# Layer 0's first stage, one k tile at a time: squares on TensorE, a third a_u head inside, and three queues ordered by hand

## The chip, the cores and the metric

The kernel runs on 1 core of one Trainium2 chip. The metric is the device time of one execution in microseconds (us). Several executions are timed, and their median is given; one more execution was recorded by the hardware profiler.

## The reference

A two-layer trunk over a latent stream x (256 tokens) and a context (256 tokens), width 2048, everything in float32. What matters here is the beginning of a layer:

```python
for l in range(DEPTH):                                   # DEPTH = 2
    shift, scale, gate = split(silu(c) @ w_mod[l] + b_mod[l], 3)        # latent
    shift_c, scale_c, gate_c = split(silu(c_ctx) @ w_mod[l] + b_mod[l], 3)   # context
    h   = rmsnorm(x,   g_pre[l]) * (1 + scale)   + shift
    h_c = rmsnorm(ctx, g_pre[l]) * (1 + scale_c) + shift_c
    proj, proj_c = h @ w_in[l], h_c @ w_in[l]            # 5120 columns: a_u a_v a_g b_q b_k b_v b_g c_x c_g
    # branch A: gelu(a_u) * (w_s-mixing of rmsnorm(gelu(a_v))) * silu(a_g)   (4 heads of 128)
    # branch B: windowed attention;  branch C: Fourier mixing;  each times its own silu gate
    y = rmsnorm(concat(branches) @ w_out[l], g_post[l])
    x = x + gate * y                                     # and the context likewise, but in the last layer
```

`rmsnorm` divides by the root of the mean of squares over the 2048 channels, plus 1e-6.

## The kernel before

**Layout.** Channels lie on the 128 partitions: x and the context together are 16 tiles `yo[k]` of 128 channels by 512 tokens (256 latent, 256 context), one for each k tile of the contraction. Products that must be accurate are done in three passes (`mm3`): both operands are split into a rounded part and the rest (`hi` by a copy on ScalarE, `lo` by a subtraction on VectorE), and hi·hi, hi·lo, lo·hi are added up in PSUM. Weights come as half tiles of 128 x 1024 f32 (512 KB) in the order of a list (`Stream`, object `W`): `W.emit` loads one into a `raw` buffer (three of them) and splits it into `whi` and `wlo` (four of each); `W.next` hands out the next one.

**Modulation.** Shift and scale of layer 0 are needed before any h. `mod_start(k0, nk)` computes them for `nk` k tiles: it loads the columns of `w_mod` that belong to them in four parts (`kg`), multiplies with silu(c) held in `cpad` (f32 products, each on 32 columns of TensorE's array, four column groups side by side, `tile_position`), transposes the result on VectorE, and sums and spreads it by four small products (`modc`). VectorE then writes scale (`gs`) and shift (`sh`). The weights of the modulation, 2 MB for a k tile, are the larger part of what the first stage loads. They lie in buffers that are free so early: `hh8`..`hl15` for pairs, `mraw macc vv mg mgl yo0`..`yo3` for single tiles.

**First stage.** `layer(0)` begins with a stage that runs over k, not over output columns, because h comes one k tile after the other: for each k, all of a_v (four blocks of 128 tokens by 512 columns, 12 products) and two heads of a_u (6 products) are added up in six PSUM banks; two further banks (`ms`) serve everything small. The eight first k tiles are taken in four pairs (`blocks`, `PAIRS`), the other eight singly. In each block: make h for its tiles (`prep_h`, `make_h`: scale on VectorE, add shift and round on ScalarE, rest on VectorE), then the products, and between them the pieces of `mod_start` of the next block.

Ahead of it: x is loaded, ScalarE squares each tile (`add_sq`), VectorE adds the squares up in `acc0`, TensorE sums over channels (`col_sums`), VectorE and GpSimd form one over the root (`rstd_cols`), VectorE makes diagonal matrices of it (`rstd_diag`), TensorE spreads it over the partitions (`bcast`), and VectorE copies it to `rb0`.

After the first stage come units (`tunit`), each a head of 128 output columns with 48 products: a_u's heads 2 and 3, then c_x, a_g, and so on. Branch A's elementwise work, the Fourier work and the attention are generators (`later`), which are stepped when a sum of modelled product times has reached their due time. The rest of the modulation (`mods`) is done on VectorE in pieces, at a rate set for each phase (`RATE`, `pace`).

**What sets the order.** TensorE's instructions are in program order (`tc.manual_schedule`); the other engines' and the load queue's order is made by a scheduler from priorities and due times.

## Time and profile before

| | |
|---|---|
| median of 3 runs | 1156.88 us (1156.8 to 1158.5) |
| the profiled execution | 1158.18 us |
| its span in the profile | 1156.4 us |
| TensorE busy (products) | 1126.6 us, 97% of the span |
| VectorE busy | 893.5 us, 77% |
| ScalarE busy | 520.0 us, 45% |
| GpSimd busy | 31.7 us, 3% |
| read from HBM | 231.08 MB, written 2.10 MB |

In the profile PE is TensorE's products, PEld its weight loads, DVE is VectorE, ACT ScalarE, POOL GpSimd, SP SyncE, whose queue issues the loads. A row of a timeline has the start and the length in us, the engine, the line of the kernel, the operation, output and inputs by the program's names, shapes, and a count (x). An f32 product appears as two records. Ends of products are modelled: starts are the surer measure. What ended an engine's idle time stands in brackets.

### The profile page before, as it was taken

To read this page: it belongs to the slowest core of one execution; us is meant where nothing else is said; L and a number is where in the kernel's file an instruction comes from. 1 tells how busy PE (TensorE), PEld (TensorE's weight loads), DVE (VectorE), ACT (ScalarE), POOL (GpSimd) and SP (SyncE) were. 2 spreads that over 40 slices of the span, in tenths; PEclk is the share of its full clock that TensorE was granted. 3 is DMA by queue.
4 is the path that set the end of the run, shared out by engine and by line. 5 is a ranking of instruction groups with operands and counts; after the bars stand their busy time and mean duration, and the time that the engine had idled before them with its cause. 6 is when DMAs were issued, how large, how long until landed. Compare 5 with 4: busy or idle time off the path is not lost.

```text
span 1156.4 us, 16569 instructions
## 1 busy us (share of the span) xinstructions
PE 1126.6 (97%) x6146; PEld 927.1 (80%) x6146; DVE 893.5 (77%) x1503; ACT 520.0 (45%) x950; POOL 31.7 (3%) x39
## 2 busy tenths in 40 slices
PE   3999999999999999999999999999999999999996
PEld 1466688888898888888888888888888988888875
DVE  5454498788988678798999897386988689868775
ACT  4222523322234676642523323366664369856442
POOL 0000000000000000000000000200500000000001
PEclk9999999999999999999999999999999999999999
DMA  9999765455665334345656665356956666556973
GB/s 341 377 391 348 258 209 164 155 182 182 212 207 182 108 104 162 102 165 181 200 164 211 221 205 194 101 164 207 219 164 202 209 209 191 173 165 205 308 251 110
DMA packets 75681, 234.27 MB, mean 203 GB/s; under 512 B 8784, under 2 KB 11984, under 8 KB 75600
## 3 DMA queue, kind: packets, MB, share of 16 engines
q1 hardware_dynamic: 73296, 231.11, 60.0%
q0 software_dynamic: 2304, 2.10, 1.2%
q8 instruction: 48, 0.79, 0.3%
q14 instruction: 33, 0.27, 0.1%
HBM read 231.08 MB, written 2.10 MB: 202 GB/s over the span
## 4 chain that ended last, share of the span: by engine, by line
PE 95%; DMA 2%; DVE 1%; ACT 1%; issue 0%; SPq 0%; POOL 0%; DVEq 0%; POOLq 0%; ACTq 0%
PE ps_t L384 15%; PE ps_t L385 15%; PE ps_t L386 15%; PE ps_t L496 11%; PE ps_t L497 5%; PE ps_mod L172 3%; PE ps_y L385 2%; PE ps_y L386 2%; PE ps_av L384 2%; PE ps_y L384 2%; PE ps_av L385 2%; PE ps_av L386 2%; PE ps_tp L759 1%; PE ps_v L386 1%; PE ps_v L384 1%; PE ps_v L385 1%
## 5 line engine op out<-in xcount | busy, mean ns | idle before, releaser
L367 ACT CAST whi<-raw 128x1024 fp32r<-128x1024 f32 x218 | 228.3, 1051 | 381.2 <-PE ps_t L385 231.1
L368 DVE TENSOR_TENSOR wlo<-raw,whi 128x1024 fp32r<-128x1024 f32 x218 | 265.0, 1219 | 76.0 <-ACT whi L367 75.0
L384 PE MATMUL ps_t<-hh,whi 128*128 128x512 f32 (+1 forms) x784 | 301.0, 384 | 0.0
L386 PE MATMUL ps_t<-hh,wlo 128*128 128x512 f32 (+1 forms) x784 | 299.4, 382 | 0.0
L385 PE MATMUL ps_t<-hl,whi 128*128 128x512 f32 (+1 forms) x784 | 299.1, 382 | 0.0
L209 DVE SCALAR_TENSOR_TENSOR macc<-mraw,cs,macc 128x512 f32<-128x512 f32 x360 | 249.5, 744 | 13.3 <-DMA mraw<-in_wmod_dram 13.1
L496 PE MATMUL ps_t<-hh,whi 128*128 128x512 f32 x512 | 185.6, 400 | 0.0
L386 PEld LDWEIGHTS ps_t<-hh,wlo 128*128 128x128 f32 x784 | 147.3, 188 | 29.3
L384 PEld LDWEIGHTS ps_t<-hh,whi 128*128 128x128 f32 x784 | 147.4, 188 | 29.1 <-issue 1.5
L385 PEld LDWEIGHTS ps_t<-hl,whi 128*128 128x128 f32 x784 | 147.4, 188 | 27.3 <-issue 0.2
L497 PE MATMUL ps_t<-hh,wlo 128*128 128x256 f32 x512 | 143.5, 280 | 0.0
L496 PEld LDWEIGHTS ps_t<-hh,whi 128*128 128x128 f32 x512 | 96.2, 188 | 21.4 <-issue 0.2
L497 PEld LDWEIGHTS ps_t<-hh,wlo 128*128 128x128 f32 x512 | 96.7, 189 | 0.3 <-issue 0.2
L463 ACT ACTIVATE hh<-w2k,sh 128x256 fp32r<-128x256 f32 x48 | 21.7, 501 | 56.6 <-DVE w2k L459 56.6
L384 PE MATMUL ps_y<-whi,hh 128*128 128x512 f32 x112 | 46.2, 412 | 0.0
L385 PE MATMUL ps_y<-wlo,hh 128*128 128x512 f32 x112 | 43.8, 392 | 0.8 <-DVE tot L905 0.8
L386 PE MATMUL ps_y<-whi,hl 128*128 128x512 f32 x112 | 43.8, 392 | 0.0
L384 PE MATMUL ps_av<-whi,hh 128*128 128x512 f32 x96 | 40.0, 417 | 0.0
L385 PE MATMUL ps_av<-wlo,hh 128*128 128x512 f32 x96 | 37.9, 395 | 0.4 <-DVE wlo L368 0.4
L172 PE MATMUL ps_mod<-hh,kt 128*32 128x512 f32 x64 | 21.6, 649 | 16.9 <-DMA hh<-in_wss_dram 16.9
L477 DVE TENSOR_TENSOR acc<-acc,w2k 128x512 f32<-128x512 f32 (+1 forms) x33 | 21.1, 641 | 18.8 <-ACT w2k L476 17.3
L401 ACT CAST w2k<-ps_tp 128x512 fp32r<-128x512 f32 x40 | 23.3, 583 | 22.0 <-PE ps_scc L385 12.0
(336 smaller groups left out, 1704.6 us busy)
## 6 DMA issues: line engine op xcount, KB each, us to landing
raw<-in_win_dram SPq DMA_DIRECT2D x160, 512.0 KB, 3.7
mraw<-in_wmod_dram SPq DMA_DIRECT2D x128, 512.0 KB, 4.2
raw<-in_wout_dram SPq DMA_DIRECT2D x64, 512.0 KB, 4.3
hh<-in_wss_dram SPq DMA_DIRECT2D x32, 256.0 KB, 5.7
hl<-in_wss_dram SPq DMA_DIRECT2D x32, 256.0 KB, 5.6
yo<-in_xT_dram SPq DMA_DIRECT2D x16, 256.0 KB, 5.3
mraw<-in_wsl_dram SPq DMA_DIRECT2D x8, 512.0 KB, 6.5
yo<-in_wsl_dram SPq DMA_DIRECT2D x16, 256.0 KB, 6.4
```

The source lines that it names most:

```text
L172: PE.matmul(ps[32 * kk:32 * kk + 32, 0:n], cpad[:, kg * 4 + kk], ws[kk], start=kg == 0, stop=kg == 3, tile_position=(0, 32 * kk))
L209: V.scalar_tensor_tensor(out=acc[:, s], in0=w[:, kk % 2], scalar=c, in1=acc[:, s], op0=ALU.mult, op1=ALU.add)
L367: A.copy(ph, r[:, c])
L368: self.last = V.tensor_tensor(out=pl, in0=r[:, c], in1=ph.bitcast(F32), op=ALU.subtract)
L384: PE.matmul(ps, st[0], mv[0], start=start, stop=False)
L385: PE.matmul(ps, st[0], mv[1], start=False, stop=False)
L386: PE.matmul(ps, st[1], mv[0], start=False, stop=stop)
L401: A.copy(hi, src)
L463: first = A.activation(h_of(l, k, sl)[0], t[:, sl], AF.Identity, bias=sh[l][:, k, s:s + 1])
L477: V.tensor_tensor(out=acc[:, sl], in0=acc[:, sl], in1=q[:, sl], op=ALU.add)
L496: PE.matmul(ps, w[0], h, start=k == 0, stop=False)
L497: PE.matmul(ps[:, 0:S], w[1], h[:, 0:S], start=False, stop=k == KT - 1)
```

## The change

- **Single tiles.** Layer 0's first stage takes all 16 k tiles singly. Modulation for k+1 is computed in step k; odd tiles below 8 use `hh14 hl14 hh15 hl15` beside `mg mgl`.
- **Third a_u head.** The unit au2 leaves the list behind the stage. Its two half tiles come inside (placed in `hh12 hl12 hh13 hl13` and `yo4`..`yo7`), and it is added up in one of the two `ms` banks: 21 products a step instead of 18. For k = 0, 1, 2 its products come together at the end of step 2. Branch A takes the three heads together, and its due times are changed.
- **Squares.** ScalarE squares each x tile, TensorE sums it over the channels (one product on 32 columns, four column groups in turn), with no addition on VectorE. The reciprocal root is spread by four products whose stationary side is one column repeated, so the diagonals go (in layer 1 too).
- **Products of zeros** (`warm`): bf16, 128 x 512, results unused: one ahead of each square's product, and groups of 2, 2, 3 and 4 up to the first step, 3 and 6 in step 0.
- **Order by hand.** VectorE, ScalarE and the load queue run in program order until the last product group of a_v at k = 14. x comes first in the queue (ahead of the constants and vectors). Loads of weights (`LOADS`) and their splits (`SPLITS`) are counted out step by step; the first split of a step is cut in two, its second part behind h. In steps 0 to 4 the modulation products lie within the step, from step 5 (`NEXT`) at its beginning.

```diff
-PAIRS, ALONE = [0, 2, 4, 6], list(range(8, KT))
+PAIRS, ALONE = [0], list(range(KT))
...
+    wz = sb([P, T], BF16, "join", 2)
+    def warm(ps, n):
+        for _ in range(n):
+            PE.matmul(ps, wz[:, 0:P], wz, start=True, stop=True)
-    def bcast(dg, n):
+    def bcast(r, n):
         ps = ms_ps("rb")
-        PE.matmul(ps[:, 0:n * P], ones, dg.rearrange("p a b -> p (a b)"), start=True, stop=True)
+        for j in range(n):
+            PE.matmul(ps[:, j * P:(j + 1) * P], r[:, j:j + 1].to_broadcast([P, P]), ident, start=True, stop=True)
...
-    NEAR = [1] * 6 + [0] * 6 + [1, 2, 3]
+    NEAR = [0] * 14 + [1, 2, 3]
+    LOADS = [1, 1, 1, 2, 1, 1, 1, 1, 1, 0, 2, 0, 1, 1, 1, 0]
+    SPLITS = [1, 1, 1, 2, 0, 1, 0, 2, 1, 1, 0, 2, 0, 1, 1, 1]
+    MIDDLE, NEXT = 3, 5
...
-        au = [mm_ps("au") for _ in range(2)]
+        au = [mm_ps("au") for _ in range(2)] + [ms_ps("au") for _ in range(1 - l)]
...
+        if l == 0:
+            for k in range(KT):
+                m = mod_start(k + 1, 1) if k + 1 < KT else iter([None] * 4)
+                def mods_next():              # modulation products of k+1, then LOADS[k] loads
...
+                def h_next():                 # modc, scale and shift, h of k+1, SPLITS[k] splits
...
+                if k % 2 == 0:
+                    take(k)
+                if k >= NEXT:
+                    mods_next()
+                    start_av(k, range(nt))
+                    if k == KT - 2:
+                        first_stage.close()
+                    h_next()
+                    if k >= KT - 2:
+                        for _ in range(2):
+                            with low(LAG), tc.issue_after(W.last.ins):
+                                next(mods)
+                    take(k, (1, 2))
+                    start_au(k)
+                elif k == 0:
+                    start_av(0, range(nt))
+                    mods_next()
+                    warm(au[2], 3)
+                    h_next()
+                    warm(au[2], 6)
+                    take(0, (1,))
+                    start_au(0, (0, 1))
+                elif k < MIDDLE:
+                    start_av(k, range(nt))
+                    take(k, (1,))
+                    start_au(k, (0,))
+                    mods_next()
+                    start_au(k, (1,))
+                    h_next()
+                    if k == 2:
+                        ws_[2] = W.next()
+                        for i in range(k + 1):
+                            start_au(i, (2,))
+                else:
+                    start_av(k, range(nt // 2))
+                    mods_next()
+                    start_av(k, range(nt // 2, nt))
+                    h_next()
+                    take(k, (1,))
+                    start_au(k)
...
-        raw = w2k([P, NFIRST])
-        DMA.dma_start(raw, const[:, 0:NFIRST])
...
-        for k in range(KT):
-            add_sq(acc0, yo[k], FULL, k == 0)
-        m = mod_start(*blocks[0])
-        next(m)
-        ps = ms_ps("rs")
-        col_sums(ps, acc0, 4)
-        dg = rstd_diag(ps[:, 0:4], 4, D)
...
+        first_stage.enter_context(tc.manual_schedule(engines={EN.DVE, EN.Activation, EN.SP}))
+        DMA.dma_start(ct, cT)
+        for k in range(KT):
+            DMA.dma_start(yo[k], xT[k])
+        raw = w2k([P, NFIRST])
+        DMA.dma_start(raw, const[:, 0:NFIRST])
+        DMA.dma_start(vecs, vec)
...
+        sq, idle = mm_ps("rs2"), mm_ps("idle")
+        for k in range(KT):
+            q = w2k([P, T])
+            A.activation(q, yo[k], AF.Square)
+            warm(idle, 1)
+            c = slice(32 * (k % 4), 32 * (k % 4) + 32)
+            PE.matmul(sq[c], ones[:, 0:32], q, start=k < 4, stop=k >= KT - 4, tile_position=(0, 32 * (k % 4)))
...
+        m = mod_start(0, 1)
+        next(m)
+        warm(idle, 2)
+        ps = ms_ps("rs")
+        for j in range(4):
+            PE.matmul(ps[:, j:j + 1], row[:, j * P:(j + 1) * P], cc("sel")[:, 0:1], start=True, stop=True)
+        r0 = rstd_cols(ps[:, 0:4], 4, D)
+        next(m)
+        warm(idle, 2)
+        rb = bcast(r0, 4)
+        rb0 = sb([P, T], F32, "acc")
+        A.copy(rb0, rb)
...
+        warm(idle, 3)
+        list(m)
+        warm(idle, 4)
```

## The prediction

> **What bounds the kernel now.** I read first the page of the profile, then the chain of waits up to 60 us, then TensorE's timeline.

> ```profile
> span 1156.4 us, 16569 instructions
> ...
> PE 95%; DMA 2%; DVE 1%; ACT 1%; issue 0%; SPq 0%; POOL 0%; DVEq 0%; POOLq 0%; ACTq 0%
> ```

> The chain of work is TensorE almost throughout. What the change touches lies ahead of that:

> ```profile
> 5.95 5.40 DMA yo<-in_xT_dram
> 11.37 5.41 DMA hh<-in_wss_dram
> 16.92 3.85 PE ps_mod L172 x8
> ...
> 31.74 5.55 PE ps_mod L172 x16
> 37.29 0.43 PE ps_av L384
> ```

> The columns are start, length, what. Until 37.3 us the chain is x arriving, the first modulation weights arriving (11.37 to 16.9), and modulation products paced by arriving weights (31.74, 5.55 us); only then does the first a_v product run. From there TensorE paces the stage:

> ```profile
> 88.43 0.50 PE L384 MATMUL ps_av<-whi,hh 128*128 128x512 f32 x1
> ...
> 91.09 0.40 PE L386 MATMUL ps_av<-whi,hl 128*128 128x512 f32 x1
> 91.42 0.24 PE L182 MATMUL ps_modc<-w2k,cst 128*32 128x4 f32 x8
> 91.60 0.50 PE L384 MATMUL ps_au<-hh,whi 128*128 128x512 f32 x1
> ...
> 92.86 0.40 PE L386 MATMUL ps_au<-hh,wlo 128*128 128x512 f32 x1
> 93.19 1.07 PE L172 MATMUL ps_mod<-mraw,kt 128*32 128x256 f32 x16
> ...
> 94.51 0.61 PE L172 MATMUL ps_mod<-vv,kt 128*32 128x256 f32 x8
> 95.05 0.50 PE L384 MATMUL ps_av<-whi,hh 128*128 128x512 f32 x1
> 95.39 0.39 PE L385 MATMUL ps_av<-wlo,hh 128*128 128x512 f32 x1
> ...
> 127.93 0.50 PE L384 MATMUL ps_av<-whi,hh 128*128 128x512 f32 x1
> ...
> 137.11 0.50 PE L384 MATMUL ps_t<-hh,whi 128*128 128x512 f32 x1
> ```

> One step over a k tile goes from one first a_v product to the next: 88.43 to 127.93 are six steps, 6.58 us each, with 18 products (12 a_v, 6 a_u) 0.23 us apart (88.43 to 91.09), the small group that spreads the modulation (91.42) and 16 modulation products (93.19 to 95.05). The stage ends at 137.11, where the unit of the third a_u head begins. No gap in these rows is a wait for data, so here more bandwidth is worth nothing, and an earlier first a_v product is worth its whole amount.

> The profiled execution took 1158.18 us, its span 1156.4; the median of the runs is 1156.88. The sum below is made on the profiled one; the forecast is 1.3 lower, for the median.

> **Work moved inside, and what is saved.** The third head adds 3 products per k tile, 48 in all, 48 x 0.23 = 11.0 us, and its unit behind the stage, also 48, goes. So TensorE's total stays, and the old stage to be compared ends at 137.1 + 11.0 = 148.1. The new step is 6.58 + 0.69 = 7.27 us; fifteen, and a last one of 21 x 0.23 = 4.8 without modulation, make 113.9 us. Two tiles of modulation that ran ahead of the first a_v product now run behind it: that is in the count.

> The order inside a step decides whether the making of h hides. From the small group to the new hi and lo parts:

> ```profile
> 20.99 1.03 PE L429 MATMUL ps_rs<-ones,acc 128*128 128x1 f32 x8
> ```
> ```profile
> 126.95 1.05 PE L172 MATMUL ps_mod<-yo,kt 128*32 128x256 f32 x16
> ...
> 130.88 0.24 PE L182 MATMUL ps_modc<-w2k,cst 128*32 128x4 f32 x8
> ```
> ```profile
> 22.05 0.16 DVE L412 TENSOR_SCALAR rs_a<-ps_rs 128x4 f32<-128x4 f32 x1 [2.97 <-PE ps_rs L429]
> ```
> ```profile
> 22.30 1.03 POOL L414 TENSOR_TENSOR rs_b<-rs_a,mhalf 128x4 f32<-128x4 f32 x1 [21.85 <-DVE rs_a L412]
> ```
> ```profile
> 143.05 0.58 ACT L401 CAST mg<-ps_mg 128x512 fp32r<-128x512 f32 x1
> ```
> ```profile
> 112.64 1.22 DVE L368 TENSOR_TENSOR wlo<-raw,whi 128x1024 fp32r<-128x1024 f32 x1
> 113.78 0.87 DVE L467 SCALAR_TENSOR_TENSOR hl<-w2k,sh,hh 128x256 fp32r<-128x256 f32 x2
> ...
> 128.07 0.45 DVE L177 STREAM_TRANSPOSE w2k<-ps_mod 128x256 f32<-128x256 f32 x1 [1.12 <-PE ps_mod L172]
> 131.19 0.16 DVE L191 SCALAR_TENSOR_TENSOR gs<-ps_modc,vecs 128x2 f32<-128x2 f32 x1 [2.68 <-PE ps_modc L182]
> ...
> 131.58 0.88 DVE L459 SCALAR_TENSOR_TENSOR w2k<-yo,gs,w2k 128x256 f32<-128x256 f32 x2
> ```

> From 130.88 (small group) scale and shift take until 131.58, the two multiplications 0.88 until 132.46. The change puts half a weight split between them and the lo part (a whole one is 1.22 us at 112.64 and delayed the lo part to 113.78; half is 0.62 by estimate): 133.08, then half of the lo part's 0.88. So the third product of the next a_v can go 2.7 us behind the small group, and an unbroken stream counts as starting 2.25 behind it. From k=5 on, 9 a_u products (2.07) and the modulation group lie between: hidden. For k=3 and 4 the 9 a_u products just do. For k=0, 1 and 2 the order puts modulation ahead of the small group: behind k=1 nothing is left, 2.05 us stand open; behind k=2 the nine postponed third-head products first wait for their own split, 1.75; behind k=0 the zero products fill, yet a_u waits for its split, and the small group for the transpose (0.7 from the end of the modulation products, 126.95 + 0.87, to 128.52), 2.2 in all. Six us of open chain; were half of it covered, 3. Stage length from the first a_v product: 113.9 + 6.0 = 119.9. So the change breaks even if the first a_v product comes at 28.2; it is at 37.3 now.

> **When the first a_v product comes.** Squares are now summed by TensorE: per x tile one product of zeros over the whole array (bf16, 512 columns) and one f32 product on 32 columns. What the latter takes:

> ```profile
> 31.64 1.02 PE L172 MATMUL ps_mod<-hh,kt 128*32 128x512 f32 x2
> ```
> ```profile
> 140.80 1.72 PE ps_mg L646 x4
> ```

> The modulation product at 31.64 is of that shape and alone: two records, 1.02 with its tail. Two f32 products of 512 columns take 1.72, 0.86 each. A one-pass product of 512 is 0.23. Going between the two shapes costs 0.10 in (92.86 to 93.19, less 0.23), 0.11 out (94.51 plus two records of 0.215, to 95.05) and up to 0.11 more on the next product (95.05 to 95.39). So a tile costs 0.86 + 0.23 + 0.2 = 1.29 us; 1.09 if going between is free, 1.41 with all of it. The four column groups, which run four modulation products in 0.43 us at 94.51, don't help here, because a product over all columns stands between any two.

> The trace has no such alternation; I take 1.29 because both shapes stand in it. [...]

> x itself comes faster than that:

> ```profile
> 1.19 0.42 SPq L96 DMA_DIRECT2D vecs<-in_vec_dram  x1
> ...
> 2.12 8.93 SPq L1054 DMA_DIRECT2D yo<-in_xT_dram  x16
> ```
> ```profile
> 5.93 0.63 ACT L473 ACTIVATE acc<-yo 128x512 f32<-128x512 f32 x1 [1.76 <-DMA yo<-in_xT_dram]
> ...
> 7.37 9.47 ACT L476 ACTIVATE w2k<-yo 128x512 f32<-128x512 f32 x14 [0.15 <-DMA yo<-in_xT_dram]
> ```

> Its squares on ScalarE run 0.68 us apart (14 in 9.47). The first square began 3.81 after its issue (2.12 to 5.93); x is now second in the queue, at 1.19, so the first square ends near 1.19 + 3.81 + 0.63 = 5.6. Sixteen tiles at 1.29 are 20.6 us, and TensorE is the slow side; ScalarE waits for it by its seven buffers.

> The clock comes on top:

> ```profile
> 24.00:25.00 1.00, 0.62 (x1) 0.50 (x2) 0.24 (x2) 0.00 (x0) 0.00 (x0) 0.61 1.03 410
> 25.00:26.00 1.00, 1.00 (x2) 0.00 (x0) 0.00 (x0) 0.46 (x1) 0.00 (x0) 0.50 1.03 404
> 26.00:27.00 1.00, 1.00 (x5) 0.20 (x8) 0.53 (x1) 0.76 (x2) 0.00 (x0) 0.50 1.04 385
> 27.00:28.00 1.00, 1.00 (x9) 0.24 (x2) 1.00 (x2) 0.87 (x1) 0.00 (x0) 0.68 1.05 387
> ```

> The third number from the end is the granted clock (behind it the share of the DMA engines and GB/s): 0.61, 0.50, 0.50, 0.68, after a pause of TensorE; it took some 3.4 us of work to come back. The modulation products of 16.92 (four in 3.85 us) were also slow. At half clock 3.4 us lose 1.7; if the work begins inside such a stretch, up to 6.8 us lose 3.4; I take 2.5. [...]

> So the squares end at 5.6 + 20.6 + 2.5 = 28.7 (at best 5.0 + 17.4 + 1.7 = 24.1, at worst 5.6 + 22.6 + 3.4 = 31.6). Behind them, in a row: copy of the sums 0.2 + 0.58 (143.05), four one-column products 1.1 (20.99), rstd on VectorE and GpSimd 1.3 (22.05 to 23.33), four products that spread it, 1.2 by the same row, two groups of modulation 1.0, transpose 0.65, hand-over 0.15, and the 2.25 above: 8.4. First a_v product: 37.1, where it was. What the single tiles gained, the squares take.

> **The sum.** 37.1 + 119.9 = 157.0 against 148.1: 8.9 us longer, 1167.1 for the profiled execution, 1165.8 for the median; as the open chain is counted in full, I say 1165.5. Ends of this case: 24.1 + 8.4 + 116.9 = 149.4 (+1.3, 1158.2) and 31.6 + 8.4 + 119.9 = 159.9 (+11.8, 1168.7).

> **Other edits, priced at nothing.** The 15 additions on VectorE, and the diagonal of rstd, go; their place is the chain above, already counted. In layer 1 one more small product replaces two VectorE multiplications, with products queued behind it. SyncE's queue is now written by hand: loads of the next weights wait in it behind modulation loads, which wait for TensorE to free their buffers; with the first a_v product this late each set has two steps, 14 us, for 2.6 MB (6.7 at the 387 GB/s of the last row above), so it is no bound; were the start early, it would be (below). Two more pieces of the later modulation per end step run on VectorE at low priority. If their cover is gone, a piece costs its own few us once.

> **Rivals.** *The squares hide.* The column groups go on running beside the zero products, the sums keep x's 0.68 us, and end near 17. [...] Then the weights decide: first modulation weights began landing at 16.92 and 1.8 MB more at 387 GB/s land at 21.6; with the last group 0.5, transpose 0.65, hand-over 0.15 and 2.25 the first a_v product is at 25.2. Steps then keep 7.27 against 6.7 of loads: end at 25.2 + 117.9, two us of open chain now lying under loads that must be awaited anyway: 143.1, 5 us sooner, 1152 (1149 to 1155). For it: every early number of the chain is a load. Against it: a product over all columns at 95.05 waited for the groups of 94.51 to end. Chance 0.24.

> *Near balance.* Clock full early, change of shape free, half of the open chain covered: 1155 to 1160. Chance 0.12: faster by over 0.2% 0.05, within 0.05, slower 0.02.

> *The clock falls again* between squares and first step, where TensorE does about 6 us of work in 8.4, as it fell at 24 after a pause: 1.7 to 3.4 more, 1169 to 1172. Chance 0.06.

> *Likeliest*, 0.58, own range 1160 to 1169.

> **The numbers.** A measurement of this kernel tells some 0.2%, 2.3 us, from no change. Faster 0.24 + 0.05 = 0.29; same 0.05; slower 0.58 + 0.02 + 0.06 = 0.66. The range 1152 to 1169.5 holds nearly all of the likeliest, all of the balance, half of the first rival and a little of the last: about 0.8.

> **What would show it.** Right: in the timeline of TensorE the f32 products of the squares come 1.2 to 1.4 us apart and end past 24 us, ScalarE's squares wait for TensorE, the first a_v product is within 33 to 40, and steps from k=5 are 7.2 to 7.3 us. Wrong: squares that keep 0.7 us apart, a first a_v product before 28, or steps under 7.

## The result, and the profile after

The changed kernel takes 1166.7 us (median of 4 runs, 1165.5 to 1166.8) against 1157.05 for the kernel before, run beside it: a ratio of 1.0078, 95% interval 1.0061 to 1.0096. It is slower by 9 to 10 us, 0.8%. In the profiled execution (1166.71 us) the span is 1164.9 against 1156.4.

The page of the profile after shows the same picture as before: TensorE carries the chain.

```profile
span 1164.9 us, 17002 instructions
...
PE 95%; DVE 2%; DMA 1%; ACT 1%; issue 1%; POOL 0%; SPq 0%; DVEq 0%; POOLq 0%; ACTq 0%
```

So the loss must stand in TensorE's own timeline. Its beginning (start, length, engine, line, operation; the bf16 products on `ps_idle` are the zeros, the f32 ones on `ps_rs` the squares), with ScalarE's squares below:

```profile
4.73 1.91 PE L1147 MATMUL ps_rs<-w2k,ones 128*32 128x512 f32 x2 [2.22 <-ACT w2k L1144]
...
9.28 1.04 PE L1147 MATMUL ps_rs<-w2k,ones 128*32 128x512 f32 x2
10.25 0.39 PE L451 MATMUL ps_idle<-join 128*128 128x512 bf16 x1
10.57 1.05 PE L1147 MATMUL ps_rs<-w2k,ones 128*32 128x512 f32 x2
...
35.05 0.49 PE L406 MATMUL ps_av<-whi,hh 128*128 128x512 f32 x1 [0.63 <-ACT hh L488]
```
```profile
18.14 0.63 ACT L1144 ACTIVATE w2k<-yo 128x512 f32<-128x512 f32 x1 [0.67 <-PE ps_rs L1147]
...
27.23 0.59 ACT L1151 COPY w2k<-ps_rs 128x512 f32<-128x512 f32 x1 [6.85 <-PE ps_rs L1147]
```

From square to square are 1.29 us (9.28 to 10.57; 1.30 on average from 9.28 to the last square at 26.15), without a break up to the copy of the sums at 27.23. From 12.95 on ScalarE waits 0.67 us for TensorE before each square (18.14 is one). The first a_v product comes at 35.05, where it was at 37.29: these 2.2 us are all that the early x, the single tiles and the squares on TensorE gained together.

Then the stage. In step 1 the small group is at 50.55 and the next a_v product at 52.33:

```profile
50.55 0.25 PE L180 MATMUL ps_modc<-w2k,cst 128*32 128x4 f32 x8
52.33 0.49 PE L406 MATMUL ps_av<-whi,hh 128*128 128x512 f32 x1 [1.53 <-ACT hh L488]
...
53.66 0.63 PE L406 MATMUL ps_av<-whi,hh 128*128 128x512 f32 x1
54.08 0.63 PE L407 MATMUL ps_av<-wlo,hh 128*128 128x512 f32 x1
```
```profile
53.00:54.00 1.00, 1.00 (x3) 0.72 (x3) 1.00 (x3) 0.70 (x2) 0.00 (x0) 0.67 0.90 279
54.00:55.00 1.00, 1.00 (x4) 0.72 (x3) 0.12 (x1) 0.00 (x0) 0.00 (x0) 0.50 0.86 328
...
56.00:57.00 1.00, 1.00 (x4) 0.74 (x4) 0.00 (x0) 0.00 (x0) 0.00 (x0) 0.63 0.99 401
```

TensorE stood 1.53 us for h, and a microsecond after it went on its clock (the third number from the end of the lower rows) was at half: a product every 0.43 us instead of 0.23, from about 53.3 to 56.7. In step 9 TensorE waits for weights, and SyncE's queue shows why they are late:

```profile
108.58 1.07 PE L170 MATMUL ps_mod<-mraw,kt 128*32 128x256 f32 x16
...
110.96 0.64 PE L170 MATMUL ps_mod<-vv,kt 128*32 128x256 f32 x8 [0.64 <-DMA vv<-in_wsl_dram]
111.53 0.50 PE L406 MATMUL ps_av<-whi,hh 128*128 128x512 f32 x1
```
```profile
91.63 0.52 SPq L678 DMA_DIRECT2D cst<-in_const_dram  x1
102.28 0.33 SPq L365 DMA_DIRECT2D raw<-in_win_dram  x1
102.70 0.85 SPq L167 DMA_DIRECT2D mraw<-in_wsl_dram  x2
...
104.12 0.39 SPq L167 DMA_DIRECT2D vv<-in_wsl_dram  x1
```

The modulation weights of tile 10 (`mraw` at 102.70, `vv` at 104.12) were issued behind a `raw` load, for which the queue stood from 92.15 to 102.28: that buffer came free only with a split in step 7. Their last part was there at 110.96, some 1.1 us after it could have been used (the modulation of a step is 1.86 long elsewhere, here 2.95, from 108.58 to 111.53). Undisturbed steps and the stage's end:

```profile
79.37 1.07 PE L170 MATMUL ps_mod<-mraw,kt 128*32 128x256 f32 x16
...
101.11 0.64 PE L170 MATMUL ps_mod<-mg,kt 128*32 128x256 f32 x8
```
```profile
157.98 0.39 PE L406 MATMUL ps_t<-hh,whi 128*128 128x512 f32 x1
```

Steps are 7.25 us (79.37 to 101.11 are three). The stage ends at 157.98, 9.9 later than the comparable 148.1 of before.

### The profile page after: what moved, and what is told of

Read it like the earlier page. It is cut to its first block, busy times and chain, and to the rows that moved or that the text cites. A ratio compares the mean times of both kernels' runs of the same rounds, so it can differ in the third digit from the quotient of the medians.

```text
span 1164.9 us, 17002 instructions
## 1 busy us (share of the span) xinstructions
PE 1144.4 (98%) x6383; PEld 936.5 (80%) x6386; DVE 881.2 (76%) x1504; ACT 522.1 (45%) x964; POOL 32.4 (3%) x39
## 4 chain that ended last, share of the span: by engine, by line
PE 95%; DVE 2%; DMA 1%; ACT 1%; issue 1%; POOL 0%; SPq 0%; DVEq 0%; POOLq 0%; ACTq 0%
PE ps_t L406 15%; PE ps_t L408 15%; PE ps_t L407 15%; PE ps_t L522 10%; PE ps_t L523 5%; PE ps_mod L170 2%; PE ps_y L407 2%; PE ps_y L408 2%; PE ps_y L406 2%; PE ps_av L406 2%; PE ps_av L407 2%; PE ps_av L408 2%; PE ps_tp L846 2%; PE ps_rs L1147 1%; PE ps_v L408 1%; PE ps_v L407 1%
## 5 line engine op out<-in xcount | busy, mean ns | idle before, releaser
L384 ACT CAST whi<-raw 128x1024 fp32r<-128x1024 f32 (+1 forms) x226 | 227.6, 1013 | 335.4 <-PE ps_t L407 223.1
L386 DVE TENSOR_TENSOR wlo<-raw,whi 128x1024 fp32r<-128x1024 f32 (+1 forms) x226 | 264.2, 1172 | 61.3 <-ACT whi L384 58.6
L406 PE MATMUL ps_t<-hh,whi 128*128 128x512 f32 (+1 forms) x768 | 294.3, 383 | 0.0
L408 PE MATMUL ps_t<-hh,wlo 128*128 128x512 f32 (+1 forms) x768 | 292.6, 381 | 0.0
L407 PE MATMUL ps_t<-hl,whi 128*128 128x512 f32 (+1 forms) x768 | 292.5, 381 | 0.0
L408 PEld LDWEIGHTS ps_t<-hh,wlo 128*128 128x128 f32 x768 | 144.4, 188 | 28.0
L406 PEld LDWEIGHTS ps_t<-hh,whi 128*128 128x128 f32 x768 | 144.4, 188 | 27.6 <-issue 1.5
L407 PEld LDWEIGHTS ps_t<-hl,whi 128*128 128x128 f32 x768 | 144.4, 188 | 26.2 <-issue 0.2
L522 PEld LDWEIGHTS ps_t<-hh,whi 128*128 128x128 f32 x512 | 96.1, 188 | 20.7 <-issue 0.2
L523 PEld LDWEIGHTS ps_t<-hh,wlo 128*128 128x128 f32 x512 | 96.8, 189 | 0.2 <-issue 0.2
L407 PE MATMUL ps_av<-wlo,hh 128*128 128x512 f32 x96 | 38.6, 402 | 0.4 <-DVE wlo L386 0.4
L175 DVE STREAM_TRANSPOSE w2k<-ps_mod 128x256 f32<-128x256 f32 x16 | 7.2, 449 | 34.1 <-PE ps_mod L170 30.7
L436 POOL TENSOR_TENSOR rs_b<-rs_a,mhalf 128x2 f32<-128x2 f32 (+1 forms) x7 | 7.3, 1041 | 811.7 <-DVE rs_a L434 811.7
```

What stands on the lines that cost most here:

```text
L384: A.copy(ph, r[:, c])
L386: self.last = V.tensor_tensor(out=pl, in0=r[:, c], in1=ph.bitcast(F32), op=ALU.subtract)
L406: PE.matmul(ps, st[0], mv[0], start=start, stop=False)
L407: PE.matmul(ps, st[0], mv[1], start=False, stop=False)
L408: PE.matmul(ps, st[1], mv[0], start=False, stop=stop)
L522: PE.matmul(ps, w[0], h, start=k == 0, stop=False)
```

## Experiments

All are the changed kernel with the edit shown. Ratios are to the kernel before, run in turn on the same chip, with their 95% intervals. As that kernel itself read 1157.8 to 1158.2 in these sets, sizes are taken from ratios (0.001 is 1.16 us), with 1.0078 for the changed kernel. Times within a profile are of one execution.

**Squares: one zero product more, and none.**

```diff
-            warm(idle, 1)
+            warm(idle, 2)
```

> The changed kernel with two products of zeros ahead of each square's product instead of one. Theory (TensorE paces the squares, a zero product is on the path): 1.30 + 0.23 = 1.53 us apart, squares end 3.5 us later, time +3.5, 1170.2 (1169.4 to 1171). Rival (x or ScalarE paces them, or the products of zeros run in the gaps): no change, 1166.7.

```diff
-            warm(idle, 1)
```

> The changed kernel without the one product of zeros ahead of each square's product; nothing else differs. Theory (the product over the whole array keeps the four column groups apart): the squares' products follow x at ScalarE's pace, 0.68 us apart instead of 1.30, the last ends near 17 to 18 instead of 27, the first a_v product comes near 26 instead of 35, and the time falls by 7 to 9 us to 1158 (1157 to 1160). Rival 1 (column groups do not run beside each other for these products either): 0.86 apart, squares end near 22, first a_v near 30, 1162. Rival 2 (the squares hide something else that is late, weights or the clock): squares end near 18, but the first a_v product stays past 32 or the steps wait for weights, 1163 to 1167.

Two zeros: 1171.07, ratio 1.0111 (1.0097 to 1.0125), 3.8 us above the changed kernel, where 3.5 was expected; the squares are 1.51 apart and the first a_v product is at 38.57, 3.52 later. None: 1156.28, ratio 0.9987 (0.9978 to 0.9995), 10.5 below the changed kernel, more than the 7 to 9 expected. From TensorE's timeline in the run without zeros, its weight loads for the squares (PEld, two for each) and the first a_v product:

```profile
5.63 0.18 PEld L1146 LDWEIGHTS ps_rs<-w2k,ones 128*32 128x32 f32 x2 [0.52 <-ACT w2k L1144]
6.31 0.18 PEld L1146 LDWEIGHTS ps_rs<-w2k,ones 128*32 128x32 f32 x2 [0.49 <-ACT w2k L1144]
...
15.32 0.14 PEld L1146 LDWEIGHTS ps_rs<-w2k,ones 128*32 128x32 f32 x2 [0.51 <-ACT w2k L1144]
16.00 0.14 PEld L1146 LDWEIGHTS ps_rs<-w2k,ones 128*32 128x32 f32 x2 [0.54 <-ACT w2k L1144]
```
```profile
26.45 0.51 PE L406 MATMUL ps_av<-whi,hh 128*128 128x512 f32 x1 [0.62 <-ACT hh L488]
```

They are 0.62 to 0.74 apart, 0.66 on average from 9.37 to 17.30, each set off by ScalarE (the releaser in brackets), even at 5.63 and 6.31, where a pass still took 0.85. So squares overlap, x's pace decides, and the first a_v product is at 26.45 instead of 35.05. The stage's end, 147.77, is 10.2 earlier: 8.6 from this, 1.6 because the clock didn't fall in this execution though the pause of 1.54 is there (the last section has where it lay). So in the changed kernel TensorE paced the squares, and a product of zeros cost its place in that row in full: the second one added 0.21 a square.

**Is it the column groups?** First the groups taken by fours instead of in turn, without zeros:

```diff
-            warm(idle, 1)
-            c = slice(32 * (k % 4), 32 * (k % 4) + 32)
...
+            c = slice(32 * (k // 4), 32 * (k // 4) + 32)
...
```

> The run without zeros between the squares, but with four x tiles after one another in the same 32 columns (k // 4) instead of in turn over the four groups (k % 4). Theory (products run beside each other only in different column groups): 0.86 us apart instead of x's 0.68, the last square ends near 20.2 instead of 18.0, 1158.4 against 1156.3 for the run without zeros (1157.7 to 1159.3). Rival (what cost was the zero product and the change of shape alone, the groups do not matter): 1156.3, squares end near 18.

1157.57, ratio 0.9998 (0.9989 to 1.0006): between the two expectations, and the interval overlaps that of the run without zeros. The time decides nothing; the first a_v product is even at 25.05, as x came sooner in that execution. The trace of the weight loads (PEld) says more:

```profile
12.61 0.11 PEld L1146 LDWEIGHTS ps_rs<-w2k,ones 128*32 128x32 f32 x1 [0.28 <-issue]
13.04 0.11 PEld L1146 LDWEIGHTS ps_rs<-w2k,ones 128*32 128x32 f32 x1 [0.32 <-ACT w2k L1144]
13.47 0.25 PEld L1146 LDWEIGHTS ps_rs<-w2k,ones 128*32 128x32 f32 x3 [0.32 <-issue]
```

Towards the end of a group the weight loads stand 0.43 apart, one by one; where the group changes (13.47) three go within 0.25: the last of the old group and two of the new one. My expectation had left out that each of the three changes lets the next square start beside the last one and wins back what the four had lost. So all sixteen in one group (`z32` holds zeros):

```diff
-            warm(idle, 1)
...
+            PE.matmul(sq[0:32], ones[:, 0:32], q, start=k == 0, stop=k == KT - 1, tile_position=(0, 0))
+            for g in range(1, 4) if k == 0 else ():
+                PE.matmul(sq[32 * g:32 * g + 32], z32, q, start=True, stop=True, tile_position=(0, 32 * g))
```

> The run without zeros between the squares, with all sixteen squares in one group of 32 columns (three small products of zeros beside the first square fill the other rows). Theory (products of one group follow each other at 0.43 us a pass, 0.86 a tile; only other groups run beside them, which the three changes of group gave the run by fours): from some 8.6 us on, where the clock is up, 0.43 between the weight loads without a break, each square falls 0.18 further behind x, the last one ends 2 to 3 us behind ScalarE's last square instead of 1.2 to 1.6, the first a_v product comes 1.5 to 2.5 later than in that run, 1158.5 (1157.5 to 1159.5). Rival (the products keep x's pace in one group too, and only the zeros cost): 1156.5, last square 1.2 to 1.6 behind ScalarE's.

The weight loads again, then ScalarE (its last square and its copy of the sums), then a row of VectorE from further on.

```profile
8.77 0.11 PEld L1147 LDWEIGHTS ps_rs<-w2k,ones 128*32 128x32 f32 x1 [0.32 <-issue]
9.19 0.11 PEld L1147 LDWEIGHTS ps_rs<-w2k,ones 128*32 128x32 f32 x1 [0.32 <-issue]
...
19.49 0.11 PEld L1147 LDWEIGHTS ps_rs<-w2k,ones 128*32 128x32 f32 x1 [0.32 <-issue]
```
```profile
15.40 0.63 ACT L1146 ACTIVATE w2k<-yo 128x512 f32<-128x512 f32 x1 [0.23 <-PE ps_rs L1147]
...
20.55 0.59 ACT L1153 COPY w2k<-ps_rs 128x512 f32<-128x512 f32 x1 [4.21 <-PE ps_rs L1147]
```
```profile
45.27 0.17 DVE L699 TENSOR_SCALAR nskb<-skb 128x8 f32<-128x8 f32 x1 [1.72 <-DMA skb<-in_sink_dram]
```

0.43 from 8.77 to 19.49 without a break, ScalarE waits for TensorE at the end (0.23 at 15.40), and the copy of the sums starts 4.5 us behind its last square: the theory, and more of it than the 2 to 3 expected. The first four passes took 0.85 each (weight loads from 4.88 to 8.30), double the later 0.43: half clock by the products, though the clock rows of the profile read 1.00 there. The first a_v product is 3.3 later than in the run by fours. The time is 1162.65, ratio 1.0046 (1.0029 to 1.0062), 4 above the expectation. Some 1 of that is the squares. The rest lies elsewhere. A small load for the attention, `skb`, and the VectorE instruction on it, at 130.6 and 141.2 in the run without zeros, have moved up to 38.6 and 45.3 in this run, ahead of the next h; why this edit moves them is open. In the profiled execution VectorE stood 1.72 us for that load (the row at 45.27), so the pause before step 2 was 2.71 us instead of 1.54, and the clock was at half for 6.8 us, 5.9 of them with products running, which is some 3 lost. So the spacing of the weight loads answers the question here, not the time.

With these four runs the 1.30 us of the change come apart: 0.86 are two passes of one group, of which other groups hide what is above 0.66 (the run without zeros); the zero product hides none of it and adds its own 0.21 to 0.23; the rest, 0.21 to 0.23, is put down to two changes of shape, which cost 0.10 and 0.11 in the profile before. That the zero product keeps the groups apart because it takes all columns, and not because its data type is another, is argued and not tried: no run had zero products on 32 columns. For the columns speaks the f32 product at 95.05 in the profile before, which waited for the groups of 94.51: it began 0.54 later, 0.11 behind their two records of 0.215.

**The old squares, with the rest of the change.**

```diff
...
-            PE.matmul(sq[c], ones[:, 0:32], q, ...)
+            add_sq(acc0, yo[k], FULL, k == 0)     # ScalarE squares, VectorE adds
...
+        col_sums(ps, acc0, 4)
```

> The changed kernel with the squares by the old way (ScalarE squares, VectorE adds, column sums by eight one-column products at the end); loads, order, third head inside and the zero products further on stay. Theory (of the whole loss the squares on TensorE are the part that can be given back at once): sums end near 17.5, first a_v product near 26 to 27 as TensorE starts at half clock, 1158 to 1160. Rival (the single-tile start is late for another reason): first a_v product past 32, 1164 to 1167.

1165.92, ratio 1.0058 (1.0044 to 1.0072). The theory was wrong on the time, which is the rival's: the interval overlaps that of the changed kernel. It was nearly right on the start: the first a_v product is at 29.11, 5.9 earlier than in the changed kernel, and some 2 of it at most are left at the end. In the timeline TensorE still works at half speed at 22 us (two zero products at 22.02 take 1.03, where such a pair at 40.26 in the changed kernel takes 0.60), and the two pauses of the changed kernel, of which one brought the clock down there, now both do, at 46.9 and 57.1:

```profile
46.38 0.50 PE L406 MATMUL ps_av<-whi,hh 128*128 128x512 f32 x1 [1.54 <-ACT hh L488]
...
47.43 0.63 PE L408 MATMUL ps_av<-whi,hl 128*128 128x512 f32 x1
...
56.84 0.58 PE L408 MATMUL ps_au<-hh,hh 128*128 128x512 f32 x1 [1.33 <-DVE hh L386]
```

With a third fall after waits for weights of 2.15 us in all near 104 to 108, the stage is 127.6 long against 122.9. In this execution the earlier start was spent on pauses that were in the order of the change anyway. It is the slowest of the five (1163.54 to 1167.73) and has the lowest mean granted clock (0.993, the others 0.994 to 0.997), so not every one need have had three falls.

**The open chain of steps 1 and 2.**

```diff
-    MIDDLE, NEXT = 3, 5
+    MIDDLE, NEXT = 1, 1
...
```

> The changed kernel with the order of the steps from k=5 on (modulation of the next tile first, then a_v, then a_u) used from k=1 on; the third head of the first three tiles stays behind a_u of k=2. Theory (open chain behind k=1 and 2 of about 2.05 + 1.75 us and the fall of the clock in step 2, 1.8 us, go): 1161 (1160 to 1163), no wait for hh between steps 1, 2 and 3, no half clock near 54. Rival (the weights of the next modulation are not there so early): TensorE waits for them in steps 1 to 3 instead, 1164 to 1167.

1161.59, ratio 1.0036 (1.0023 to 1.0049), 4.9 below the changed kernel. The third head of tiles 0 to 2 stays behind step 2. TensorE doesn't wait for h or for weights in steps 1 to 4, and the clock stays up; first a_v product 35.16, stage 118.1 instead of 122.9. As the theory had it.

**The pause or the clock?** The pause left as long, but filled:

```diff
                     h_next()
+                    if k == 1:
+                        warm(au[2], 7)
```

> The changed kernel with seven products of zeros behind the making of h in step 1, where TensorE waits 1.53 us for the h of tile 2; the wait stays as long, but TensorE is busy in it. Theory (that pause, falling in one stretch of the clock gate, brings the half clock of 53.25 to 56.66): the clock stays up in step 2 and the time falls by 1.8 to 1164.9 (1164.3 to 1165.6). Rival (the fall comes from elsewhere, or the next pause of 1.33 us in step 2 takes it over): 1166.5 to 1167.

1165.56, ratio 1.0072 (1.0058 to 1.0086): the intervals overlap, the timing leaves it open. The stretch that the expectation names is, as measured, the 3.41 us from 49.92 to 53.33 in which the changed kernel's pause lies (last section). In the profiled execution (1164.72) the clock stays up (1.00 in every microsecond from 26 to 74) and the stage is 121.4 instead of 122.9. The mean granted clocks of all executions agree: 0.996 in the four of the changed kernel, 0.997 or 0.998 in the six with the wait filled. So the pause of 1.5 us cost some 1.5 us twice, and filling it saved the second in the trace; that the whole kernel gets faster by it is not shown.

**The queue.**

```diff
-    SPLITS = [1, 1, 1, 2, 0, 1, 0, 2, ...
+    SPLITS = [1, 1, 1, 2, 0, 1, 1, 1, ...
```

> The changed kernel with one weight split moved from step 7 to step 6 (SPLITS 0, 2 becomes 1, 1), so that the load which waits for its buffer, and with it the modulation loads of the next tiles queued behind it on SyncE, go out some 7 us sooner. Theory (order of that queue, not its bandwidth, made the wait of about 1.1 us near 110): the wait is gone, 1165.6 (1164.9 to 1166.2). Rival (the loads are late because the transfers are full): the wait stays or stands elsewhere, 1166.7.

1165.59, ratio 1.0064 (1.0052 to 1.0076); the intervals overlap. So the gain in time is not shown. The trace shows the cause plainly: the `raw` load goes out 7 us sooner, the modulation behind it is whole again (108.92 to the next a_v at 110.78), and the stage is 1.1 shorter. Rows of SyncE's queue and of TensorE's timeline:

```profile
95.37 0.33 SPq L365 DMA_DIRECT2D raw<-in_win_dram  x1
95.79 0.85 SPq L167 DMA_DIRECT2D mraw<-in_wsl_dram  x2
```
```profile
108.92 1.07 PE L170 MATMUL ps_mod<-mraw,kt 128*32 128x256 f32 x16
...
110.78 0.50 PE L406 MATMUL ps_av<-whi,hh 128*128 128x512 f32 x1
```

**The third head outside again.**

```diff
-                    if l == 0: a.insert(3 - i, half("au2", 0, i)) ...
-            for j in heads[:3 - l]:
+            for j in heads[:2]:
...
-            yield 11.0 if l == 0 else 7.0
+            yield 12.0 if l == 0 else 7.0
```

> The changed kernel with the third a_u head as a unit of its own behind the stage again (its two half loads and splits taken from the lists, the due times of the later branch as before the change); zero products, squares and order stay. Theory (the head inside costs nothing and covers the chain and the loads): stage shorter by 11 and a unit of 11 behind it; as a step of 6.6 us covers less, 0.9 each opens in steps 3 and 4 and loads of 2.6 MB are as long as a step: 1167 to 1172, 1169 likeliest. Rival (the head inside costs: its postponed products, its splits): 1163 to 1166.

1171.53, ratio 1.011 (1.0096 to 1.0125), 3.7 above the changed kernel: within the range. The pause before h is now there behind step 2 too, with the clock falling twice:

```profile
51.61 0.51 PE L403 MATMUL ps_av<-whi,hh 128*128 128x512 f32 x1 [1.54 <-ACT hh L485]
...
61.63 0.50 PE L403 MATMUL ps_av<-whi,hh 128*128 128x512 f32 x1 [1.53 <-ACT hh L485]
```

But the stage's end with 11 for the unit behind it, 147.59 + 11, is only 0.6 later than 157.98, and the second fall of the clock alone is worth some 1.7. The rest of the profiled execution's 4.7 us, some 4, lies behind the stage, where among others TensorE waits 2.0 us between 150 and 200 for copies of the Fourier work (1.5 on ScalarE, 0.5 on VectorE). The due times that I set back may be why; that was not tried apart. As an undoing of the head alone the run is not clean; that the head inside costs nothing is supported, that it gains 4 is not.

**The three mended, and two versions of it.** No zeros between squares, `NEXT = 1`, the one split moved:

> No zero products between the squares, modulation first from k=1 on, and the one split moved, all three in the changed kernel. Theory (the three losses add up): 1166.7 - 10.4 (run without zeros) - 5.1 (run with modulation first) - 1.1 (queue) = 1150.1 (1149 to 1152), 7 us faster than before, first a_v product near 26.5 and the stage's end near 143. Rival (with the early start the weights decide): TensorE waits for modulation weights in steps 1 to 6, 1153 to 1157.

1151.46, ratio 0.9944 (0.9932 to 0.9956): 6.5 us faster than the kernel before, and within the range expected. TensorE's waits up to 160 us in this run, all of them, in us, times and the longest; then its first a_v product and the end of its stage:

```profile
PE ps_rs L1150 <- ACT w2k L1148: 4.5, 1, 4.5
PE ps_av L406 <- ACT hh L488: 0.6, 1, 0.6
PE ps_rb L457 <- POOL rs_b L436: 0.3, 1, 0.3
```
```profile
25.36 0.50 PE L406 MATMUL ps_av<-whi,hh 128*128 128x512 f32 x1 [0.62 <-ACT hh L488]
```
```profile
142.19 0.39 PE L406 MATMUL ps_t<-hh,whi 128*128 128x512 f32 x1
```

After the first a_v product none is left. The stage is 116.8 long. The rival, weights that come too late, did not appear, though the share of the DMA engines was 0.94 to 1.07 in every microsecond from 26 to 73.

```diff
+        m1 = mod_start(1, 1)      # in place of warm(idle, 4); its last part behind make_h(0)
```

> The three mended, and the modulation of tile 1 moved ahead of the first a_v product in place of the zero products there and behind it. Theory (the open chain of step 0, 2.2 us, goes under the wait for the first h): 1 to 2 us below the run with the three mended, 1148.5 (1147.5 to 1150). Rival (the weights of tile 1 land after 26, or those of tile 2 after 31, so the wait only changes its name): equal to the run with the three mended within 0.7, or slower.

1151.01, ratio 0.9942 (0.9928 to 0.9955), not to be told from the last. The stage is 3 us shorter, and the first a_v product 2.4 later (27.74): TensorE's products on the weights of tile 1 start between 24.5 and 27.2, as these land. The rival's first half.

With the old squares (`add_sq`) in place of the squares without zeros:

> The run with the old squares, and with modulation first from k=1 on and the one split moved. Theory (the first run with the old squares lost its early start to three stretches of half clock and to the queue, all behind pauses that this order doesn't have): first a_v product near 29, stage's end near 147, 1155.3 (1154.5 to 1156.5), that is some 3.8 above the run with the three mended, as TensorE's first work runs at half clock. Rival (TensorE's idle first 17 us bring the clock down again later): 1157 to 1162.

1156.57, ratio 0.9988 (0.998 to 0.9997), its profiled execution 1154.43. No clock fall in the stage, which is 116.8 long, as with the three mended; it starts at 28.66, 3.3 us later. The median is 5.1 above the run with the three mended by the ratios, and I expected 3.8; the runs reach from 1154.4 to 1159.4, and why is open. The squares on TensorE are worth having, once nothing stands between them.

## Why the prediction was right

The forecast was 1165.5, the median is 1166.7, and the likeliest case is the one that came. Its steps, one after the other:

- **The squares are paced by TensorE**: 1.29 forecast, 1.30 measured, for the reason given (0.86 + 0.23 + shape); the four runs on squares show the pacing and the first two terms, and what these leave (0.21 to 0.23) fits the third. The sums end at 27.0 (0.2 ahead of the copy at 27.23), not 28.7: the first square came 0.9 sooner than taken, half clock cost 2.0 and not 2.5 (it lasted 4.2 us, from the first square at 4.73 to 8.96, where a zero product goes from 0.61 to 0.39), and the sixteenth tile has no zero product behind it.
- **The chain behind them**: 8.4 forecast; from 27.0 to an unbroken stream (the third product, at 35.90, less two places of 0.23) 8.4. First a_v product forecast 37.1 on that reckoning, measured 35.4. It is the squares' term that was 1.7 too long; this one was right.
- **The step**: 7.27 forecast, 7.25 measured.
- **The open chain**: 6.0 forecast for steps 0 to 2. From 35.05 to step 3's first product at 64.70 are 29.65; less three steps of 7.25 and 1.7 for the clock, 6.2 are left. The run with modulation first removes steps 1 and 2 and the fall of the clock: 4.8 of stage length. The run with the three mended, which has only step 0 left of it, has a stage of 116.8, where 113.9 + 2.2 = 116.1 follows from the forecast.
- **"Loads no bound"** was right for bandwidth and wrong for order. I had SyncE's queue waiting for TensorE's buffers; it waited for a `raw` buffer, that is, for a split. 1.1 us.
- **The clock** was to fall, if at all, between squares and first step (chance 0.06). It stayed up there, with the zeros; it fell in step 2, behind the pause of step 1, which I had counted (2.05 forecast for the open chain) but not as a reason for a second loss. 1.7 us.
- **The end**: 157.0 forecast, 157.98 measured; 1.7 too late at the start, then 1.1 and 1.7 too little in the stage. Two misses of opposite sign hid each other; that the stage's end came out within 1 us is partly luck.
- **What came after**: +9.9 at the stage's end are +8.0 at the layer boundary and +8.5 at the end. The forecast had nothing for that, so the time too is closer than the steps deserve. These are the products that spread rstd there, in both kernels:

```profile
740.24 0.45 PE ps_rb L433 x2
```
```profile
748.27 0.46 PE ps_rb L457 x4
```

TensorE has no wait of note between the stage and that point in either kernel, so the 1.9 us lie in how its products follow each other. They are lost bit by bit: the same product comes 9.8 later in the changed kernel at the start of the Fourier work (190.76 against 180.99), 9.3 at the first attention scores (378.98 against 369.69), 8.4 at 726.27 against 717.85. What shortens the rows is open.

The first rival, squares at x's pace, failed on its condition, not on its price: the groups do not go on beside the zero products. Where that product is taken away, the first a_v product is at 26.45 (25.2 in the rival's sum) and the time about that of the kernel before; its 1152 left the open chain, the clock and the queue out of account, and with these mended the runs give 1151.5. That the groups run beside each other where nothing stands between them, the runs without zeros show (0.66 us a square where one group alone needs 0.86); with the zero product between them it was 1.30.

## What to carry to other kernels

Filler that is to keep the clock up belongs where the engine would wait (seven zero products in the wait of 1.53 us: clock at 1.00, stage 121.4 instead of 122.9), never inside a row that the engine itself paces (the run without zeros between the squares is 10.5 us shorter): price it there like any other instruction (0.21 to 0.23), with the change of shape on both sides (0.10 and 0.11 here). When work is moved so that a chain lies open, count a pause of 1.5 us twice, once as itself and once as the chance of half a clock behind it (here six of eight such pauses were followed by 3.41 us at half clock, a loss of 1.7); reordering that covers the pause was worth more than its length (modulation first: pauses of 1.53 and 1.33 us gone, stage 4.8 shorter). In a queue ordered by hand, ask for each load which buffer it waits for and what is behind it.

## What the hardware showed that I had not expected

**The clock fell after pauses of 1.5 us, and not every time.** Over the profiled executions of these kernels, a pause of 1.53 or 1.54 us in steps 1 to 3, with TensorE busy on both sides, was followed by a fall in six of eight cases, one of 1.33 in one of nine; each fall lasted 3.41 us, at a granted clock of 0.50, and the one pause of 2.71 brought 6.83. The pause of 1.54 in the run without zeros, up to 43.73, went without it; of the window rows below the first is from there, the others from the run with one group (the clock is the third number from the end):

```profile
44.00:45.00 1.00, 1.00 (x4) 0.55 (x4) 1.00 (x4) 1.00 (x3) 0.00 (x0) 1.00 1.03 418
```
```profile
46.00:47.00 1.00, 0.19 (x1) 0.19 (x1) 1.00 (x3) 0.75 (x2) 0.00 (x0) 0.50 0.98 397
...
52.00:53.00 1.00, 1.00 (x4) 0.64 (x3) 0.00 (x0) 0.00 (x0) 0.00 (x0) 0.63 0.04 16
```
